# Sums of weight blocks by copies and adding transfers instead of VectorE, in a two-layer decoder trunk

## The chip, the cores and the metric

One core of a Trainium2 chip runs the whole program. The metric is the device time of one execution in microseconds, as the median of several; the kernel before took 2176.65 us (median of 3 runs, 2176.36 to 2177.28). Lower is better. The engines are TensorE (matrix products into PSUM), VectorE and ScalarE (elementwise work), GpSimd, and SyncE, whose queue (SP) issues most transfers. All of a core's transfers run on the same 16 DMA engines.

## The reference, cut to what matters

The program is a trunk of two layers on 1024 tokens of width 1024, in float32. Layer 0 mixes tokens with a gated linear recurrence, layer 1 with stick-breaking attention. Each is followed by a SwiGLU network of inner width 2816, which is the part that this change touches:

```python
def swiglu_ffn(x, w_in, w_out):
    gu = jnp.einsum("bsd,df->bsf", x, w_in)
    h = jax.nn.silu(gu[..., :D_FF]) * gu[..., D_FF:]
    return jnp.einsum("bsf,fd->bsd", h, w_out)
```

Here x is the normalized stream, `w_in` is 1024 x 5632 (gate columns, then up columns) and `w_out` is 2816 x 1024.

## The kernel before

Every float32 operand is split into a high part (a cast to float32r, by ScalarE) and a low part (the rest, by a subtraction on VectorE). A product is three matmuls: high x high, high weight x low input, low weight x high input (`mm3`, lines 141 to 144).

Both products of the network are computed by a Strassen-Winograd scheme (`mix_out_ffn_in`, line 625): inputs and weights are cut into 2 x 2 blocks, and seven products of sums of blocks replace eight. The sums on the input side are formed once per layer in `v_steps` (line 579). The sums on the weight side are formed for each step anew. A step of the first product ("f" step, f = 0 to 21) makes 128 gate columns and the 128 up columns that go with them, for all tokens. Then 13 steps ("v" steps) make the second product.

The class `Weights` (line 668) holds one step's weights. `load_a` and `load_b` bring two raw tiles of 512 KB, ra and rb, from HBM, on SP. Each has two halves: a1 and a2 in ra, b1 and b2 in rb, 128 partitions x 512 columns. The raw tiles come from a pool of three buffers, so the next load waits until an old tile has had its last reader. From the halves come four sums, kept in one buffer each for s1 and s4 and a double-width one for sb, whose halves are called c1 and c2 below:

- `s12` (line 695): s1 = b1 + b2
- `s2` (line 698): c1 = s1 - a1
- `s3` (line 701): c2 = a1 - b1
- `do_s4` (line 704): s4 = c1 - a2

`a_hi`, `b_hi`, `c_hi`, `d_hi` cast the high parts (wah from ra, wbh from sb, wch from s1 and b2, wd from s4) and `a_lo` to `d_lo` subtract for the low parts.

A step runs the seven products in the order 0, 1, 2, 3, 4, 6, 5 (`ORDER`, line 565), four blocks of three matmuls each. Product 0 and 1 use wa, 2 and 4 use wb, 3 and 5 use wc, 6 uses wd. In the f steps from 4 to 19 product 1 is itself done by a smaller scheme of the same kind (`inner_part`), on pairs of steps, whose weight sums `inner_sums` takes from two raw tiles. Each product is evicted from PSUM as it ends (`post`), and the gate (`gate`) and the input sums of the second product (`operands`) follow. The loop of the steps begins at line 1192. In it, w is the step's own weights, nw the next step's, ahead those of the step after. After product k of a step it does, besides evictions:

- before product 0: the low part of w's sb, the high part of s1 and b2
- k = 0: their low parts; k = 2: w's wd, and nw's wah
- k = 3: nw's s1; k = 4: nw's wal, c1, c2; k = 5: nw's wbh and s4
- k = 1 or 3: load of ahead's ra; k = 5: load of ahead's rb

TensorE, ScalarE, VectorE and GpSimd run in the written order in this part of the program. The order on SP is the scheduler's. A queue is served in its order, so an instruction that waits holds those behind it.

Of the kernel before, what the change touches and what calls it, by code (L numbers as in the profile page):

```python
# [12 lines left out]
AF = mybir.ActivationFunctionType  # L13
ALU = mybir.AluOpType
# [15 lines left out]
V_MIX, V_FFN, V_FIN, V_BIN, V_CW, V_CB, V_GB, V_LAM, V_BO = 0, 16, 32, 40, 56, 88, 96, 112, 120  # L30
# [3 lines left out]
def trunk(  # L34
# [21 lines left out]
    nc = tc.nc  # L56
    f32 = lambda t: t.bitcast(F32)
# [38 lines left out]
    vc = cp.tile([P, P], F32, name="vc")  # L96
# [15 lines left out]
    def load_raw(src, shape):  # L112
        raw = rp.tile([P, D], F32, tag="raw", name="raw")
        view = raw if len(shape) == 1 else raw.rearrange("p (a b) -> p a b", a=shape[0])
        nc.sync.dma_start(view, src)
        return raw
# [11 lines left out]
    def cols(w, c0, n=P):  # L128
        return w[:, c0 : c0 + n].rearrange("(k p) c -> p k c", p=P)
# [120 lines left out]
    half = lambda t, n: t[:, n * NB : (n + 1) * NB]  # L250
# [8 lines left out]
    with ExitStack() as st, tc.manual_schedule(engines={E.PE, E.Activation, E.DVE, E.Pool, E.SP}):  # L259
# [49 lines left out]
        ps = pst("vps0")  # L309
# [71 lines left out]
        for r0, r1 in ((0, 32), (32, 64), (64, P)):  # L381
            ps = pst("vps")
            nc.tensor.transpose(ps[:, 0 : r1 - r0], vall[r0:r1, :], ident[r0:r1, r0:r1])
            nc.vector.tensor_copy(vc[:, r0:r1], ps[:, 0 : r1 - r0])
        broadcast_r(sps, "tp", 0)
        row_factors(1)
        wsplit(2)
# [191 lines left out]
    def v_steps(h, v, j, gcol, ta, tb):  # L579
        g1, g2 = (vc[:, gcol + d : gcol + d + 1] for d in (j, j + HK))  # L580
        h11, h12, h21, h22 = h[j][0], h[j][1], h[j + HK][0], h[j + HK][1]
        V = nc.vector
        b12 = rbc[0]

        def direct(i, src, g):
            hi, lo = v[i, j]
            nc.scalar.activation(hi, src, AF.Copy, scale=g)
            V.scalar_tensor_tensor(lo, src, g, f32(hi), op0=ALU.mult, op1=ALU.subtract)

        def summed(i, t):  # L590
            hi, lo = v[i, j]
            nc.scalar.copy(hi, t)
            V.tensor_sub(lo, t, f32(hi))
# [9 lines left out]
        V.scalar_tensor_tensor(tb, h22, g2, ta, op0=ALU.mult, op1=ALU.add)  # L603
        summed(3, ta)
        yield
        summed(2, tb)

        V.scalar_tensor_tensor(ta, h22, g2, b12, op0=ALU.mult, op1=ALU.subtract)
        yield
        summed(4, ta)  # L610
        yield

        V.scalar_tensor_tensor(ta, h21, g2, tb, op0=ALU.mult, op1=ALU.subtract)
        yield
        summed(5, ta)

    def v_last(h, v, j, gcol):
        g2 = vc[:, gcol + j + HK : gcol + j + HK + 1]
# [6 lines left out]
    def mix_out_ffn_in(mix, bias, layer, gnext, outs):  # L625
        w_in = ffn_w_in[layer]
        gcol = V_FFN + layer * ND
        V = nc.vector
        half = lambda t, i: t[:, i * NB : (i + 1) * NB]
# [3 lines left out]
        ta, tb = (sp_.tile([P, NB], F32, name=x) for x in ("ta", "tb"))  # L633
# [34 lines left out]
        class Weights:  # L668
            def __init__(self, load, m=HK, eng=V):
                self.load, self.m, self.eng, self.a = load, m, eng, {}  # L670
                self.ready = False

            def load_a(self):
                self.ra = self.load(0)
# [12 lines left out]
                for i, x in zip(idx, range(2)):  # L687
                    self.a[i] = (half(hi, x), half(lo, x))

            def s12(self):  # L690
# [3 lines left out]
                self.s1, self.s4 = (t[:, 0 : self.m * P] for t in (self.s1, self.s4))  # L694
                self.eng.tensor_add(self.s1, self.part(self.rb, 0), self.part(self.rb, 1))

            def s2(self):
                self.eng.tensor_sub(self.part(self.sb, 0), self.s1, self.part(self.ra, 0))

            def s3(self):  # L700
                self.eng.tensor_sub(self.part(self.sb, 1), self.part(self.ra, 0), self.part(self.rb, 0))  # L701

            def do_s4(self):
                self.eng.tensor_sub(self.s4, self.part(self.sb, 0), self.part(self.ra, 1))

            def a_hi(self):
                self.wa = wtile("wah")
# [45 lines left out]

        def weights_in(f, now=True):
            w = Weights(lambda x: load_raw(cols(w_in, x * DFF + f * P), (ND,)))
            if now:
                w.load_a()
                w.load_b()
            return w
# [11 lines left out]
        with tc.manual_schedule(engines={E.PE, E.Activation, E.DVE, E.Pool}):  # L771
# [11 lines left out]
            w = None  # L783
            for j in range(HK):
                rows = (j, j + HK)
                dn = [(d, n) for d in rows for n in range(NH)] if j else [(d, n) for n in range(NH) for d in rows]
                for k, (d, n) in enumerate(dn):
                    o = HK * j + k
                    if (d, n) in begun:
                        ps = begun[d, n]  # L790
                        hi, lo = mix.w[d]
                        mm3(ps, hi[:, ND - 1], lo[:, ND - 1], xh[ND - 1][n], xl[ND - 1][n], False, True)
                    else:
                        ps = pp.tile([P, NB], F32, tag="p", name="ob_ps")
# [11 lines left out]
                    if o == 10:  # L806
                        w = weights_in(0)
# [40 lines left out]
            def post0(i, ps):  # L848
                g0, g1, u0, u1 = halves(0)
                if i == 0:  # L850
                    nc.scalar.copy(g1, ps)
                elif i == 1:
                    V.tensor_add(g0, ps, g1)
                elif i == 2:
                    V.tensor_add(g1, ps, g1)
                elif i == 4:
                    V.tensor_add(u0, ps, g1)
                elif i == 3:
                    V.tensor_sub(u1, u0, ps)
                    V.tensor_sub(g1, g1, ps)  # L860
                elif i == 5:
                    V.tensor_add(u0, ps, u0)
                else:
                    V.tensor_sub(g1, g1, ps)

            def post(f, i, ps):
                g0, g1, u0, u1 = halves(f)
                if i == 0:  # L870
                    nc.scalar.copy(g0, ps)
                elif i == 1:
                    V.tensor_add(g0, ps, g0)
                elif i == 2:
                    nc.scalar.copy(g1, ps)
                elif i == 3:
                    nc.scalar.copy(u1, ps)
                elif i == 4:
                    nc.scalar.copy(u0, ps)
                    V.tensor_sub(u1, u0, u1)  # L880
                elif i == 6:
                    V.tensor_sub(g1, g1, ps)
                else:
                    nc.scalar.copy(u0, ps)

            def gate(f, k):
                G, U = GT[f % 2], UT[f % 3]
                if k == 0:
                    V.tensor_mul(G, ob, G)
                elif k == 1:  # L890
                    nc.scalar.activation(G, G, AF.Silu)
                elif k == 2:
                    V.tensor_mul(G, ob, G)
                else:
                    V.tensor_mul(U, U, G)
# [111 lines left out]
            ps = half(ob, 0)  # L1007
# [184 lines left out]
            for s_, (kind, x) in enumerate(steps):  # L1192
                w, nw, ahead = nw, nxt, None
# [23 lines left out]
                for k, i in enumerate(ORDER):  # L1217
# [61 lines left out]
                    if k == 0:  # L1279
                        if kind == "v":  # L1280
                            w.c_hi()
                        w.c_lo()
                    elif k == 2:
                        w.d_hi()
                        w.d_lo()
                        if nw:
                            nw.a_hi()
                    elif nw and last_two:
                        if k == 4:
                            nw.a_lo()  # L1290
# [543 lines left out]
```

## Time and profile before

| | before |
|---|---|
| median of 3 runs | 2176.65 us |
| the profiled execution | 2176.2 us |
| its span in the profile | 2174.1 us |
| clock granted to TensorE | 0.999 |
| GpSimd busy | 113.5 us |
| moved by DMA | 294.49 MB, 135 GB/s |

The first products of the network (f = 0 to 21) start on TensorE at 325 us in layer 0 and at 1527 us in layer 1; the v steps start at 726 and 1928 us. The rows that carry the argument are shown with the prediction. In a row of groups stand line, engine, operation, output <- inputs, partitions x elements and type, count, then busy us, mean ns of one, and idle time before it with what ended it. In a row of the timeline stand start and duration in us, engine, line, operation. In a row of transfers the last figure is the median time in us from issue to landing. "SPq" is SP's queue, "PEld" TensorE's weight loads.

### The profile page before, as it was taken

Reading aid. Unit: us, or ns where it says so; the run is one execution under the profiler, and the core shown is the slowest. Engines: PE = TensorE matmul, PEld = TensorE weight load, DVE = VectorE, ACT = ScalarE, POOL = GpSimd, SP = SyncE. Lnnn points to the kernel's source line nnn. Section 1 sums busy time; section 2 is a strip of 40 time slices with the busy share of each in tenths; the row PEclk is TensorE's granted clock in tenths of the full one; section 3 lists DMA queues with packets and bytes.
Section 4 is the critical chain, followed back from the end, with each engine's and each line's share of the span. In section 5 each row is a group of like instructions: output and inputs, shape, how many; then the busy total and the mean of one; then the engine's idle time right before and its main releaser. Section 6 shows DMA issues by size and latency. Waiting matters only on the chain.

```text
span 2174.1 us, 28371 instructions
## 1 busy us (share of the span) xinstructions
PE 2160.4 (99%) x10414; PEld 1810.7 (83%) x10414; DVE 1787.3 (82%) x2604; ACT 1104.9 (51%) x1821; POOL 113.5 (5%) x85
## 2 busy tenths in 40 slices
PE   8999999999999999999999999999999999999998
PEld 7888888888888888888888888888888888888887
DVE  7887778888888887887888888886888888888886
ACT  6667445444444544564555555553544444454556
POOL 1222020000000000000000000001000000000002
PEclk9999999999999999999999999999999999999999
DMA  7111422334345864434333344463133444587442
GB/s 234 49 49 39 160 88 67 113 126 158 132 152 197 271 219 131 146 120 101 101 94 93 99 105 107 139 211 117 59 114 115 154 141 154 172 276 237 136 154 93
DMA packets 305323, 294.49 MB, mean 135 GB/s; under 512 B 16280, under 2 KB 212000, under 8 KB 305184
## 3 DMA queue, kind: packets, MB, share of 16 engines
q1 hardware_dynamic: 305024, 292.42, 42.8%
q8 instruction: 81, 1.33, 0.2%
q14 instruction: 58, 0.48, 0.1%
q10 hardware_dynamic: 160, 0.27, 0.0%
HBM read 184.09 MB, written 83.36 MB: 123 GB/s over the span
## 4 chain that ended last, share of the span: by engine, by line
PE 90%; DVE 5%; ACT 3%; DMA 1%; issue 0%; SPq 0%; DVEq 0%; ACTq 0%
PE p_ps L142 17%; PE p_ps L144 17%; PE p_ps L143 17%; PE qk_ps L142 4%; PE qk_ps L144 4%; PE qk_ps L143 4%; PE wt_ps L1650 3%; PE ob_ps L143 3%; PE ob_ps L142 2%; PE ob_ps L144 2%; PE z_ps L1620 2%; PE z_ps L1621 2%; PE av_ps L1672 2%; PE av_ps L1671 1%; PE i_ps L144 1%; PE i_ps L143 1%
## 5 line engine op out<-in xcount | busy, mean ns | idle before, releaser
L142 PE MATMUL p_ps<-vh,wbh 128*128 128x512 f32 x524 | 204.7, 391 | 0.0
L143 PE MATMUL p_ps<-vl,wbh 128*128 128x512 f32 x524 | 204.5, 390 | 0.0
L142 PE MATMUL p_ps<-vh,wch 128*128 128x512 f32 x524 | 204.2, 390 | 0.0
L144 PE MATMUL p_ps<-vh,wcl 128*128 128x512 f32 x524 | 204.1, 390 | 0.0
L144 PE MATMUL p_ps<-vh,wbl 128*128 128x512 f32 x524 | 204.1, 390 | 0.0
L143 PE MATMUL p_ps<-vl,wch 128*128 128x512 f32 x524 | 203.9, 389 | 0.0
L1659 ACT CAST th<-wt_ps 128x512 fp32r<-128x512 f32 x192 | 92.5, 482 | 209.0 <-PE wt_ps L1650 208.9
L717 ACT CAST wbh<-sb 128x1024 fp32r<-128x1024 f32 (+2 forms) x69 | 69.8, 1012 | 190.4 <-DVE sb L701 190.4
L1660 DVE TENSOR_TENSOR tl<-wt_ps,th 128x512 fp32r<-128x512 f32 x192 | 106.2, 553 | 62.8 <-ACT th L1659 60.9
L144 PE MATMUL p_ps<-vh,wal 128*128 128x512 f32 x396 | 154.3, 390 | 0.1
L143 PE MATMUL p_ps<-vl,wah 128*128 128x512 f32 x396 | 154.1, 389 | 0.0
L142 PE MATMUL p_ps<-vh,wah 128*128 128x512 f32 x396 | 154.1, 389 | 0.0
L142 PE MATMUL qk_ps<-vh,whi 128*128 128x512 f32 x264 | 118.3, 448 | 0.0
L144 PEld LDWEIGHTS p_ps<-vh,wbl 128*128 128x128 f32 x524 | 98.4, 188 | 21.8 <-DVE wbl L721 0.8
L144 PEld LDWEIGHTS p_ps<-vh,wcl 128*128 128x128 f32 x524 | 98.3, 188 | 21.1 <-DVE wcl L731 0.6
L142 PEld LDWEIGHTS p_ps<-vh,wch 128*128 128x128 f32 x524 | 98.4, 188 | 20.6 <-ACT tb L1176 0.2
L143 PEld LDWEIGHTS p_ps<-vl,wch 128*128 128x128 f32 x524 | 98.4, 188 | 20.2
L142 PEld LDWEIGHTS p_ps<-vh,wbh 128*128 128x128 f32 x524 | 98.6, 188 | 19.0
L143 PEld LDWEIGHTS p_ps<-vl,wbh 128*128 128x128 f32 x524 | 98.6, 188 | 18.5
L1636 DVE TENSOR_TENSOR_SCAN w<-w,unit 128x128 f32<-128x128 f32 (+3 forms) x128 | 108.3, 846 | 4.1 <-ACT w L1633 4.1
L144 PE MATMUL qk_ps<-vh,wlo 128*128 128x512 f32 x264 | 104.1, 394 | 0.0
L143 PE MATMUL qk_ps<-vl,whi 128*128 128x512 f32 x264 | 103.5, 392 | 0.0
(390 smaller groups left out, 5929.6 us busy)
## 6 DMA issues: line engine op xcount, KB each, us to landing
raw<-in_ffn_w_in SPq DMA_DIRECT2D x88, 512.0 KB, 3.9
vl<-pd SPq DMA_DIRECT2D x128, 256.0 KB, 3.3
pd<-U SPq DMA_DIRECT2D x90, 256.0 KB, 2.3
kk<-two SPq DMA_DIRECT2D x64, 256.0 KB, 4.2
raw<-in_ffn_w_out SPq DMA_DIRECT2D x56, 256.0 KB, 3.4
raw<-in_attn_w_qkv SPq DMA_DIRECT2D x24, 512.0 KB, 4.1
h<-hd SPq DMA_DIRECT2D x32, 256.0 KB, 5.4
hd<-h SPq DMA_DIRECT2D x32, 256.0 KB, 2.0
```

Of the source, the lines that this page charges most:

```text
L142: nc.tensor.matmul(ps, lhsT=wh, rhs=mh, start=first, stop=False, **kw)
L143: nc.tensor.matmul(ps, lhsT=wh, rhs=ml, start=False, stop=False, **kw)
L144: nc.tensor.matmul(ps, lhsT=wl, rhs=mh, start=False, stop=last, **kw)
L717: nc.scalar.copy(self.full(self.wb), self.full(self.sb))
L1620: nc.tensor.matmul(ps[:, 0 : c1 - c0], lhsT=lhsT, rhs=KK[q][hx][:, 0, c0:c1], start=True, stop=False)
L1621: nc.tensor.matmul(ps[:, 0 : c1 - c0], lhsT=lhsT, rhs=KK[q][hx][:, 1, c0:c1], start=False, stop=True)
L1636: nc.vector.tensor_tensor_scan(rev, rev, unit[:, NB - n :][:, ::-1], 0.0, op0=ALU.mult, op1=ALU.add)
L1650: nc.tensor.transpose(tp[:, c : c + P], W[q, hx, j, kb // 4][:, (kb % 4) * P : (kb % 4 + 1) * P], ident)
L1659: nc.scalar.copy(th[:, q0:], tp[:, q0:])
L1660: nc.vector.tensor_sub(tl[:, q0:], tp[:, q0:], f32(th)[:, q0:])
L1671: nc.tensor.matmul(ps[:, q0:], lhsT=VV[q][:, kb, hx], rhs=th[:, q0:], start=first, stop=False)
L1672: nc.tensor.matmul(ps[:, q0:], lhsT=VV[q][:, kb, hx], rhs=tl[:, q0:], start=False, stop=last)
```

## The change

For the f steps from 2 to 21 the four sums are no longer formed on VectorE. `by_dma` (after product 0 of the step before) has SP copy a1 into both halves of sb, and b1 into s1. Then three transfers issued by GpSimd, which add to their destination, make c2 += b1, s1 += b2 and c1 += s1. `by_dma4` (after product 2) has SP copy a2 into s4, and GpSimd add c1 to it. Since only additions occur, c1, c2 and s4 have other signs than before: c1 = s1 + a1, c2 = a1 + b1, s4 = c1 + a2. Signs elsewhere make up for this: the norm gains of the network are negated once (so the input side and the gate come with the other sign), two of the input sums are stored negated, subtractions after some products become additions, and SiLU is taken with scale -1. The steps f = 0 and f = 1 form their sums on VectorE with the new signs, the v steps as before. In the built program VectorE has 2421 instructions in place of 2581, GpSimd 226 in place of 65, SP 1041 in place of 877, ScalarE 1785 in place of 1784; TensorE's count is the same.

```diff
+        nc.scalar.activation(vc[:, V_FFN:V_FIN], vc[:, V_FFN:V_FIN], AF.Copy, scale=-1.0)
...
-        def summed(i, t):
+        def summed(i, t, minus=False):
             hi, lo = v[i, j]
+            if minus:
+                nc.scalar.activation(hi, t, AF.Copy, scale=-1.0)
+                V.scalar_tensor_tensor(lo, t, -1.0, f32(hi), op0=ALU.mult, op1=ALU.subtract)
+                return
             nc.scalar.copy(hi, t)
             V.tensor_sub(lo, t, f32(hi))
...
-        summed(2, tb)
+        summed(2, tb, True)
...
-        summed(5, ta)
+        summed(5, ta, True)
...
+            def by_dma(self):
+                self.sums()
+                dma = nc.gpsimd.dma_start
+                a1, b1, c1 = (half(t, 0) for t in (self.ra, self.rb, self.sb))
+                b2, c2 = half(self.rb, 1), half(self.sb, 1)
+                nc.sync.dma_start(c1, a1)
+                nc.sync.dma_start(c2, a1)
+                nc.sync.dma_start(self.s1, b1)
+                dma(c2, b1, accum_op=ALU.add)
+                dma(self.s1, b2, accum_op=ALU.add)
+                dma(c1, self.s1, accum_op=ALU.add)
+
+            def by_dma4(self):
+                nc.sync.dma_start(self.s4, half(self.ra, 1))
+                nc.gpsimd.dma_start(self.s4, half(self.sb, 0), accum_op=ALU.add)
...
             def s2(self):
-                self.eng.tensor_sub(self.part(self.sb, 0), self.s1, self.part(self.ra, 0))
+                (self.eng.tensor_add if self.plus else self.eng.tensor_sub)(
+                    self.part(self.sb, 0), self.s1, self.part(self.ra, 0)
+                )
...
-                    V.tensor_sub(u1, u0, u1)
+                    V.tensor_add(u1, u0, u1)
                 elif i == 6:
-                    V.tensor_sub(g1, g1, ps)
+                    V.tensor_add(g1, ps, g1)
...
-                    nc.scalar.activation(G, G, AF.Silu)
+                    nc.scalar.activation(G, G, AF.Silu, scale=-1.0)
...
                         w.c_lo()
+                        if nw and nw.plus:
+                            nw.by_dma()
                     elif k == 2:
                         w.d_hi()
                         w.d_lo()
+                        if nw and nw.plus:
+                            nw.by_dma4()
...
-                        if k == 3:
+                        if k == 3 and not nw.plus:
                             nw.s12()
                         elif k == 4:
                             nw.a_lo()
-                            nw.s2()
-                            nw.s3()
+                            if not nw.plus:
+                                nw.s2()
+                                nw.s3()
                         elif k == 5:
                             nw.b_hi()
-                            nw.do_s4()
+                            if not nw.plus:
+                                nw.do_s4()
```

More of the change, by code (lines that the diff above doesn't have):

```diff
@@ L670, in __init__ @@
                 self.load, self.m, self.eng, self.a = load, m, eng, {}
-                self.ready = False
+                self.ready, self.plus = False, False
             def load_a(self):
@@ L688, in put, with sums @@
                     self.a[i] = (half(hi, x), half(lo, x))
-            def s12(self):
+            def sums(self):
                 self.sb = sp_.tile([P, S], F32, tag="sb", name="sb", bufs=1)
@@ L694, in s12 @@
                 self.s1, self.s4 = (t[:, 0 : self.m * P] for t in (self.s1, self.s4))
+            def by_dma(self):
[12 more added lines that the diff above has]
+                nc.gpsimd.dma_start(self.s4, half(self.sb, 0), accum_op=ALU.add)
+            def s12(self):
+                self.sums()
                 self.eng.tensor_add(self.s1, self.part(self.rb, 0), self.part(self.rb, 1))
             def s2(self):
-                self.eng.tensor_sub(self.part(self.sb, 0), self.s1, self.part(self.ra, 0))
+                (self.eng.tensor_add if self.plus else self.eng.tensor_sub)(
+                    self.part(self.sb, 0), self.s1, self.part(self.ra, 0)
+                )
             def s3(self):
-                self.eng.tensor_sub(self.part(self.sb, 1), self.part(self.ra, 0), self.part(self.rb, 0))
+                (self.eng.tensor_add if self.plus else self.eng.tensor_sub)(
+                    self.part(self.sb, 1), self.part(self.ra, 0), self.part(self.rb, 0)
+                )
             def do_s4(self):
-                self.eng.tensor_sub(self.s4, self.part(self.sb, 0), self.part(self.ra, 1))
+                (self.eng.tensor_add if self.plus else self.eng.tensor_sub)(
+                    self.s4, self.part(self.sb, 0), self.part(self.ra, 1)
+                )
             def a_hi(self):
@@ L755, in weights_in @@
             w = Weights(lambda x: load_raw(cols(w_in, x * DFF + f * P), (ND,)))
+            w.plus = True
             if now:
@@ L858, in post0 @@
                 elif i == 3:
-                    V.tensor_sub(u1, u0, ps)
-                    V.tensor_sub(g1, g1, ps)
+                    V.tensor_add(u1, ps, u0)
+                    V.tensor_add(g1, ps, g1)
                 elif i == 5:
@@ L863, in post0 @@
                 else:
-                    V.tensor_sub(g1, g1, ps)
+                    V.tensor_add(g1, ps, g1)
             def post(f, i, ps):
@@ L879, in post @@
                     nc.scalar.copy(u0, ps)
-                    V.tensor_sub(u1, u0, u1)
+                    V.tensor_add(u1, u0, u1)
                 elif i == 6:
-                    V.tensor_sub(g1, g1, ps)
+                    V.tensor_add(g1, ps, g1)
                 else:
```

## The prediction

> **What bounds the kernel now.** I read the page's busy table first, then the stretches of time in which the w_in steps run, then TensorE's own waits, then one such step instruction by instruction.
>
> ```profile
> span 2174.1 us, 28371 instructions
> PE 2160.4 (99%) x10414; PEld 1810.7 (83%) x10414; DVE 1787.3 (82%) x2604; ACT 1104.9 (51%) x1821; POOL 113.5 (5%) x85
> ```
> ```profile
> 360.00:749.00 389.00, 389.00 (x1881) 328.63 (x1880) 329.26 (x489) 181.38 (x284) 0.00 (x0) 1.00 0.47 155
> 1530.00:1925.00 395.00, 394.93 (x1915) 333.67 (x1914) 332.39 (x496) 181.37 (x280) 0.00 (x0) 1.00 0.42 139
> ```
>
> The second fence gives, per stretch, the busy time of TensorE, its weight loads, VectorE, ScalarE and GpSimd, then the granted clock, the DMA share and GB/s. The two stretches are the w_in steps of the two layers. TensorE has no gap, VectorE is busy 85%, GpSimd does nothing.
>
> ```profile
> 1664.16 0.39 PE L142 MATMUL p_ps<-vh,wah 128*128 128x512 f32 x1
> 1664.39 0.39 PE L143 MATMUL p_ps<-vl,wah 128*128 128x512 f32 x1
> 1666.88 0.28 PE L142 MATMUL i_ps<-ith,ish 128*128 128x256 f32 x1
> 1682.66 0.39 PE L142 MATMUL p_ps<-vh,wah 128*128 128x512 f32 x1
> 1686.82 0.40 PE L142 MATMUL p_ps<-vh,wbh 128*128 128x512 f32 x1
> ```
> ```profile
> PEld p_ps L144 <- DVE wal L712: 1.0, 2, 0.5
> PEld p_ps L144 <- DVE wbl L721: 0.8, 2, 0.4
> PEld p_ps L144 <- DVE wcl L731: 0.6, 2, 0.4
> ```
>
> These are starts in TensorE's timeline. The first product of a step is 12 matmuls in 1666.88 - 1664.16 = 2.72 us, 0.227 us each; one step starts at 1664.16, the next at 1682.66. "Busy" could hide gaps, since ends are modelled, but an even pitch of starts can't. In all the span weight loads waited 2.4 us for VectorE's low parts, in six places. So there is next to nothing to win here: VectorE isn't the bound, and the question is whether the new path is quick enough to stay hidden.
>
> **What is removed.** Twenty w_in steps per layer (f 2 to 21; f 0 and 1 keep VectorE) lose four operations each, 160 in all.
>
> ```profile
> L695 DVE TENSOR_TENSOR s<-raw 128x512 f32<-128x512 f32 x58 | 40.5, 698 | 0.0
> L704 DVE TENSOR_TENSOR s<-sb,raw 128x512 f32<-128x512 f32 x58 | 39.9, 687 | 0.0
> L698 DVE TENSOR_TENSOR sb<-s,raw 128x512 f32<-128x512 f32 x58 | 39.8, 686 | 0.1
> L701 DVE TENSOR_TENSOR sb<-raw 128x512 f32<-128x512 f32 x58 | 39.8, 685 | 0.0
> ```
>
> 40 x (0.698 + 0.687 + 0.686 + 0.685) = 110 us less on VectorE. On the path that sets the end it is worth 0, by TensorE's even pitch; at most the 2.4 us above.
>
> **The signs.** They change operations, not counts or shapes: subtractions into additions, a copy into a scaled copy. Sixteen low parts (L593, 0.69 us) become scalar_tensor_tensor (0.75 us by L603), 16 x 0.06 = 1 us of VectorE, hidden by TensorE; without that cover it is 1 us. The negated gains cost one small ScalarE operation near the start (0.3 us by the 128x4 activation). Both at 0.
>
> ```profile
> L603 DVE SCALAR_TENSOR_TENSOR tb<-h,vc,ta 128x512 f32<-128x512 f32 x8 | 6.0, 746 | 0.1
> L593 DVE TENSOR_TENSOR vl<-tb,vh 128x512 fp32r<-128x512 f32 x8 | 5.5, 693 | 0.7
> L180 ACT ACTIVATE rs_s<-ssum,eps 128x4 f32<-128x4 f32 x2 | 0.6, 299 | 0.0
> ```
>
> **What is added: a chain of transfers.** Per step SP issues copies c1, c2, s1 after product 0 and s4 after product 2; GpSimd issues c2 += b1, s1 += b2, c1 += s1, s4 += c1. All are 256 KB. What is summed in step f is used in step f + 1. s1 copy, s1 += b2, c1 += s1 follow each other, and only then is sb whole; s4 += c1 is a fourth link. The next step's c1 overwrites sb, which s4 += c1 reads, so SP waits for it: four links make a loop that must fit into one step. No accumulating transfer stands in the trace, so I price it from the nearest rows.
>
> ```profile
> kk<-two SPq DMA_DIRECT2D x64, 256.0 KB, 4.2
> vl<-pd SPq DMA_DIRECT2D x128, 256.0 KB, 3.3
> hd<-h SPq DMA_DIRECT2D x32, 256.0 KB, 2.0
> raw<-in_ffn_w_in SPq DMA_DIRECT2D x88, 512.0 KB, 3.9
> g<-hd SPq DMA_DIRECT2D x32, 256.0 KB, 5.6
> q1 hardware_dynamic: 305024, 292.42, 42.8%
> ```
> ```profile
> L379 POOL COPY vall<-vraw 128x128 f32<-128x128 f32 x1 | 0.3, 291 | 7.4 <-DMA vraw<-in_lru_b_out 7.4
> 1664.44 0.38 SPq L115 DMA_DIRECT2D raw<-in_ffn_w_in  x1
> 1660.15 1.22 DVE L712 TENSOR_TENSOR wal<-raw,wah 128x1024 fp32r<-128x1024 f32 x1
> 1697.89 1.22 DVE L712 TENSOR_TENSOR wal<-raw,wah 128x1024 fp32r<-128x1024 f32 x1
> 1681.11 1.06 ACT L717 CAST wbh<-sb 128x1024 fp32r<-128x1024 f32 x1 [3.10 <-DVE sb L701]
> 1685.06 1.22 DVE L721 TENSOR_TENSOR wbl<-sb,wbh 128x1024 fp32r<-128x1024 f32 x1
> ```
>
> Step length: the two L712 rows lie two steps apart, (1697.89 - 1660.15)/2 = 18.87 us. One accumulate: 4.2 us (kk<-two, the only SBUF to SBUF transfer of this size), plus a second read, since the destination is an operand too: 42.8% of 2174.1 us for 292.42 MB is 0.83 us per 256 KB; plus 0.3 us of GpSimd to start it (L379). Sum 5.3 us. Bounds: 2.0 (hd<-h, a lone transfer) and 8.4 (kk<-two twice). I take 5.3, as kk<-two is the nearest in kind. From c1's issue to s1 landed: two more issues of 0.4 and 3.3 (vl<-pd, issued in series) = 4.1; bounds 2.8 and 5.0 with 2.0 and 4.2 for the landing.
>
> Loop: 4.1 + 3 x 5.3 = 20.0 us against 18.87: 1.13 us too long per step. By the low bounds it is 2.8 + 6.0 = 8.8 us and costs nothing, by the high ones 5.0 + 25.2 = 30.2 and every step would be 11 us longer. Slack before TensorE notices: rb lands at 1664.44 + 3.9 = 1668.34, s1 at 1671.64, sb at 1682.24. wbh is wanted at 1686.82 and wbl two matmuls later, 1687.28; less 1.06 (L717) and 1.22 (L721), sb may come at 1685.0. Slack 2.8 us per layer. Loss: 2 x (20 x 1.13 - 2.8) = 39.6 us.
>
> Queued behind the new waits. On SP, behind c1: the next load of raw weights (wanted by the inner sums at product 3), s4, the stores of U and its sums, the load of rb for the step after; they are all late only if the loop is. On GpSimd: nothing (0.00 busy above). On ScalarE, behind wbh: the eviction of product 6 and wch, then on VectorE wcl, which frees s1. Moved earlier: the load of rb no longer waits for the L704 subtraction, only for L712; worth 1 us at most of the slack.
>
> VectorE's entries in the steps between 1660 and 1700 us are TENSOR_TENSOR throughout, like the L712 and L721 rows. The Trainium skill, "SBUF — State Buffer", section "Who interferes with whom", warns that a DMA of GpSimd's queue starves while VectorE runs in a 2-port mode, but names copies, casts and tensor_scalar for it. By that rule these steps pay nothing for it; if it held for TENSOR_TENSOR it would be the third rival below.
>
> **Sum.** 2176.2 us was the profiled run (span 2174.1 plus 2.1 around it), 0.45 below the median 2176.65. 2176.65 + 39.6 = 2216 us.
>
> **Rivals.**
> 1. The chain fits: not slower. The point is an accumulate of (18.87 - 4.1)/3 = 4.92 us, only 0.4 below my value; hd<-h at 2.0 speaks for it, kk<-two at 4.2 with a second read against. Then TensorE keeps its pitch: 2176.5 us. The Trainium skill, "DMA: Bandwidth & Descriptors", section "Anatomy of one DMA — SWDGE (gpsimd) path", fits 2.0 us + bytes/436e3 for this queue; with both operands read that is an estimate of 3.2 us, and the loop 13.7 us. No run here shows that queue.
> 2. The 16 DMA engines become the bound. Share 0.47 x 18.87 = 8.9 us a step, plus four copies of 0.83, plus four accumulates of three passes, 10.0: 22.2 us, 3.3 too long: 40 x 3.3 - 5.6 = 126 us, 2303 us. With two passes it is 18.9, just even. Against it: 0.83 is a mean with many small packets.
> 3. Each accumulate's start waits for a VectorE instruction, up to 1.22 us (L712): accumulate 6.5, loop 23.6, 4.7 too long: 182 us, 2359 us.
> 4. Only the layer's last steps lose, where 16 reloads of h (g<-hd, 32 in two layers, 5.6 us to landing where 3.3 is usual) pass the same engines: three of 0.83 before each of two accumulates is 5.0 us against 2.8 of slack: 2 x 2.2, 2181 us.
> 5. Faster: all 2.4 us of the weight loads' waits vanish and something like it elsewhere: 2174 us. VectorE's relief speaks for it, the even pitch against.
>
> **How the numbers follow.** The chain is too long: 0.50, of which 0.08 lies above 2400 (an accumulate over 6.8 us; at 8.4 the loop is 29.3 and the time 2588). Rival 1: 0.29. Rival 2: 0.08. Rival 3: 0.06. Rival 4: 0.04. Rival 5: 0.03. Prediction 2216 us. The forecast's own range is 2181 to 2400; with rival 1 it becomes 2174 to 2400. 0.2% is 4.4 us, about what a measurement of this kernel can tell from no change. Slower: 0.50 + 0.08 + 0.06 + 0.04 = 0.68; same 0.29; faster 0.03.
>
> **What would show it.** Right: gaps in TensorE ahead of wbh in most w_in steps, wbh (ScalarE) waiting for a DMA into sb, SP waiting for s4 += c1, a step near 20 us. Rival 1: an even 0.227 us pitch and accumulates landing under 4.9 us. Rival 2: a DMA share near 1. Rival 3: accumulates starting as VectorE's instructions end. VectorE must lose 160 instructions and some 110 us in any case. I am wrong if TensorE keeps its pitch, or if the gaps lie elsewhere than ahead of wbh and the products after it.

## The result, and the profile after

The changed kernel takes 2269.09 us (median of 4 runs, 2262.33 to 2272.12) against 2176.51 us (median of 4, 2176.04 to 2177.28) for the kernel before: ratio 1.0421, 95% interval 1.0396 to 1.0445, slower by some 93 us. The profiled execution took 2262.33 us, 86.1 more than the one of before. One figure above is wrong: the v steps of the kernel before start on TensorE at 745 and 1947 us; 726 and 1928 us are the starts of f = 21.

From the page of the kernel after, the span, the busy table and GpSimd's DMA queue (packets, MB, share of the 16 engines' span); then its stretches (busy time of TensorE, weight loads, VectorE, ScalarE, GpSimd, granted clock, DMA share, GB/s) for the step f = 2, the steps 3 to 18 and the step 20 of layer 0; then its waits (engine, line waited for: us in total, times, longest).

```profile
span 2260.6 us, 29098 instructions
PE 2187.9 (97%) x10414; PEld 1823.0 (81%) x10414; DVE 1695.0 (75%) x2444; ACT 1096.1 (48%) x1822; POOL 252.4 (11%) x245
q0 software_dynamic: 23040, 41.95, 11.1%
```
```profile
365.10:391.60 26.50, 22.08 (x86) 17.25 (x85) 16.61 (x21) 12.42 (x18) 4.38 (x5) 0.87 0.61 165
391.60:718.90 327.30, 309.17 (x1484) 259.65 (x1483) 220.37 (x325) 131.34 (x207) 54.13 (x62) 0.99 0.84 227
740.80:768.10 27.30, 21.16 (x85) 16.99 (x85) 12.73 (x16) 7.75 (x12) 4.35 (x5) 0.87 0.94 297
```
```profile
PE p_ps L142 <- ACT G L902: 52.4, 29, 6.1
ACT wbh L747 <- DMA sb<-s: 268.8, 40, 13.3
SPq L706 <- DMA s<-sb: 188.1, 36, 8.6
POOL sb L711 <- DMA s<-raw: 215.5, 40, 9.2
```

TensorE, without a gap before, now stands still in the w_in steps. Of the 86 us, some 59 are idle time (span minus busy: 72.7 us against 13.7) and 27.5 are a longer busy time, most of it matmuls that last longer at a lower granted clock (0.87 in the first and the last of these rows). The waits name the links. wbh waits in all 40 steps for the adding transfer that ends c1 (sb<-s), c1's own transfer waits in all 40 for s1, and SP's copy for the next step waits in 36 for s4 += c1 (s<-sb). That last line is the loop. VectorE lost its 160 instructions, but 92 us of busy time rather than 110.

TensorE's own wait carries the name of an eviction (ScalarE, line 902). One turn of the kernel after in its timeline shows why. (Lines after: 706 c1 copy, 710 s1 += b2, 711 c1 += s1, 715 s4 += c1, 747 wbh, 756 and 757 wch, 902 the eviction of product 0.)

```profile
522.90 0.47 SPq L706 DMA_DIRECT2D sb<-raw  x1
...
528.01 0.89 POOL L710 DMA_DIRECT2D s<-raw  x1
534.78 0.87 POOL L711 DMA_DIRECT2D sb<-s  x1 [5.88 <-DMA s<-raw]
538.71 1.05 ACT L747 CAST wbh<-sb 128x1024 fp32r<-128x1024 f32 x1 [8.02 <-DMA sb<-s]
539.26 0.86 POOL L715 DMA_DIRECT2D s<-sb  x1 [3.61 <-DVE G L920]
...
540.14 0.62 ACT L756 CAST wch<-s 128x512 fp32r<-128x512 f32 x1
540.66 0.62 ACT L757 CAST wch<-raw 128x512 fp32r<-128x512 f32 x1
541.18 0.59 ACT L902 COPY G<-p_ps 128x512 f32<-128x512 f32 x1
541.82 0.50 PE L142 MATMUL p_ps<-vh,wbh 128*128 128x512 f32 x1 [2.14 <-ACT G L902]
543.66 0.47 SPq L706 DMA_DIRECT2D sb<-raw  x1
```

The turn from one c1 copy to the next takes 543.66 - 522.90 = 20.76 us: 5.11 us to s1 += b2, 6.77 for that link, 4.48 for c1 += s1 up to the start of s4 += c1, 4.40 for s4 += c1. When sb is whole at last, ScalarE works off its queue in order (wbh, an eviction, wch twice), and only then product 0's eviction, which frees the PSUM bank that product 2 uses again: 541.82 - 538.71 = 3.1 us after sb. The line that a wait names is the last in a row of things, not the first.

The same copies at the start and the end of seventeen turns of each layer, from the timeline of the kernel after:

```profile
376.03 0.47 SPq L706 DMA_DIRECT2D sb<-raw  x1
...
728.27 0.47 SPq L706 DMA_DIRECT2D sb<-raw  x1
...
1624.14 0.47 SPq L706 DMA_DIRECT2D sb<-raw  x1
...
1969.43 0.47 SPq L706 DMA_DIRECT2D sb<-raw  x1
```

(728.27 - 376.03)/17 = 20.72 us in layer 0 and (1969.43 - 1624.14)/17 = 20.31 us in layer 1, 20.52 in the mean, against a step of 18.87 us before.

### The profile page after: what moved, and what is told of

It is laid out like the page before. It is cut to its first block, busy times and chain, and to the rows that moved or that the text cites. A ratio compares the mean times of both kernels' runs of the same rounds, so it can differ in the third digit from the quotient of the medians.

```text
span 2260.6 us, 29098 instructions
## 1 busy us (share of the span) xinstructions
PE 2187.9 (97%) x10414; PEld 1823.0 (81%) x10414; DVE 1695.0 (75%) x2444; ACT 1096.1 (48%) x1822; POOL 252.4 (11%) x245
## 3 DMA queue, kind: packets, MB, share of 16 engines
q0 software_dynamic: 23040, 41.95, 11.1%
## 5 line engine op out<-in xcount | busy, mean ns | idle before, releaser
L142 PE MATMUL p_ps<-vh,wbh 128*128 128x512 f32 x524 | 215.0, 410 | 52.4 <-ACT G L902 52.4
L144 PE MATMUL p_ps<-vh,wbl 128*128 128x512 f32 x524 | 211.5, 404 | 4.7 <-DVE wbl L751 4.7
L143 PE MATMUL p_ps<-vl,wbh 128*128 128x512 f32 x524 | 211.2, 403 | 0.0
L751 DVE TENSOR_TENSOR wbl<-sb,wbh 128x1024 fp32r<-128x1024 f32 (+2 forms) x69 | 83.1, 1205 | 108.9 <-ACT wbh L747 107.6
L143 PEld LDWEIGHTS p_ps<-vl,wbh 128*128 128x128 f32 x524 | 102.4, 195 | 19.7
```

Source lines behind the costliest of these rows:

```text
L142: nc.tensor.matmul(ps, lhsT=wh, rhs=mh, start=first, stop=False, **kw)
L143: nc.tensor.matmul(ps, lhsT=wh, rhs=ml, start=False, stop=False, **kw)
L144: nc.tensor.matmul(ps, lhsT=wl, rhs=mh, start=False, stop=last, **kw)
L751: V.tensor_sub(self.full(lo), self.full(self.sb), self.full(f32(self.wb)))
```

## The experiments

The table compares each kernel's steps with those of the kernel before, from its profiled execution: the length of a step is the time between the first matmuls of product 0 in it and in the next, and the figures are the sums of what is over, both layers together. The first columns are medians and ratios to the kernel before, with 95% intervals.

| kernel | us | ratio (95%) | f = 2 | f = 3 to 19 | f = 20 | f = 21, v |
|---|---|---|---|---|---|---|
| after | 2269.09 | 1.0421 (1.0396 to 1.0445) | 14.3 | 50.6 | 15.0 | 6.8 |
| e1_signs_only | 2176.43 | 0.9999 (0.9990 to 1.0009) | 0 | 0 | 0 | 0 |
| e2_mid_only | 2240.39 | 1.0297 (1.0280 to 1.0314) | 0 | 57.4 | 0 | 0 |
| e3_unlinked | 2208.55 | 1.0145 (1.0130 to 1.0160) | 13.9 | 8.5 | 6.1 | 0 |
| e4_s1_first | 2237.64 | 1.0273 (1.0251 to 1.0296) | 14.1 | 34.6 | 14.1 | 0.2 |
| e5_wch_later | 2270.76 | 1.0439 (1.0424 to 1.0455) | 13.6 | 54.8 | 16.7 | 9.7 |
| e6_no_adding | 2179.75 | 1.0021 (1.0012 to 1.0031) | 1.7 | 0 | 0 | 1.8 |
| e7_c2_vector | 2205.25 | 1.0139 (1.0124 to 1.0154) | 11.1 | 5.6 | 6.2 | 3.8 |
| e8_combined | 2185.69 | 1.0050 (1.0035 to 1.0065) | 0 | 9.4 | 0 | 0 |
| e9_s4_only | 2190.87 | 1.0068 (1.0053 to 1.0083) | 0 | 15.5 | 0 | 0 |
| e10_s4_vector | 2195.53 | 1.0087 (1.0071 to 1.0102) | 8.3 | 0 | 7.0 | 4.4 |
| e11_two_links | 2176.93 | 1.0006 (0.9996 to 1.0015) | 0 | 0 | 0 | 0 |
| e12_s4_plain | 2178.42 | 1.0009 (0.9999 to 1.0019) | 0 | 1.6 | 0 | 0 |

**The signs alone.** All sums go back to VectorE, the new signs stay: a flag of its own, in all five conditions of the loop, decides on the transfers.

```diff
+            w.dma = False
...
-                        if nw and nw.plus:
+                        if nw and nw.dma:
                             nw.by_dma()
...
-                            if not nw.plus:
+                            if not nw.dma:
                                 nw.s2()
                                 nw.s3()
```

> The four sums back on VectorE, with the new signs; no copies or adding transfers. Theory (the whole loss is the chain of transfers): the time of before, 2176.5 us within 1, no wait of TensorE in the w_in steps. Rival (the sign edits or the negated gains cost part of the 92 us): clearly above 2180 us.

It measured as the kernel before. The signs cost nothing that shows, and the whole loss belongs to the transfers.

**The middle steps alone.** The same flag with `w.dma = 3 <= f <= 19`: the first and the last steps keep VectorE.

> Transfers for the weights of f = 3 to 19 only; f = 2, 20 and 21 form their sums on VectorE. In the changed kernel's trace the steps f = 2 are 7 us longer than before in each layer, f = 20 and 21 and the first v step together some 11 us. Theory (these ends are lost on top of the loop): about 36 us less than the changed kernel, near 2233 us, with the steps in between as long as they were. Rival (the ends only collect a delay that the loop in between has built up): the loss stays above 80 us, near 2260 us.

The losses of f = 2, 20 and 21 vanish, those of the middle stay (57.4 against 50.6). The time is 7 us above the theory's 2233 and 20 below the rival's 2260. The kernel after is 29 us slower than this one, so the ends are worth some 29 us of the 93. The last steps are no alternative to the slow loop, as the prediction's fourth rival had it; they come on top.

**One link cut.** s4's adding transfer takes b1, not c1, so that it need not wait for c1 and the next c1 copy need not wait for it; every byte still moves.

```diff
-                nc.gpsimd.dma_start(self.s4, half(self.sb, 0), accum_op=ALU.add)
+                nc.gpsimd.dma_start(self.s4, half(self.rb, 0), accum_op=ALU.add)
```

> The last adding transfer adds b1 to s4 in place of c1, so the output is another, but every transfer keeps its size and place. The next copy into sb no longer waits for it. Theory (a loop of four links, 20.4 us, against a step of 18.87): SP's wait ahead of the copies into sb vanishes, sb comes about 15.5 us after the step's start and the steps f = 3 to 19 lose nothing; only the ends stay, 2210 to 2225 us. Rival (the 16 DMA engines, at a share of 0.80 to 0.96, are the bound): the bytes are the same, so the time stays at 2260 to 2270 us.

The wait of this kernel that answers to the first of the kernel after:

```profile
PE p_ps L142 <- ACT G L902: 15.1, 12, 3.0
```

The middle loses 8.5 us in place of 50.6 with the same transfers on the same engines; the theory had nothing for it, and its 2210 us are missed by 1.5. So the middle is for the most part the loop's, not the DMA engines': from 391 to 719 us they are busier here (share 0.90) than in the kernel after (0.84 in the row above). In five of the eight waits that are left in the middle (f = 9, 11, 13 and 17), the eviction of product 0 had itself waited for a store of G; the run with only s4 by transfers, below, comes back to it.

**The links in another order.** s1 is copied first, and s1 += b2 goes ahead of c2 += b1.

```diff
+                nc.sync.dma_start(self.s1, b1)
                 nc.sync.dma_start(c1, a1)
                 nc.sync.dma_start(c2, a1)
-                nc.sync.dma_start(self.s1, b1)
-                dma(c2, b1, accum_op=ALU.add)
                 dma(self.s1, b2, accum_op=ALU.add)
+                dma(c2, b1, accum_op=ALU.add)
                 dma(c1, self.s1, accum_op=ALU.add)
```

> The same transfers in another order: s1 is copied first, s1 += b2 is issued ahead of c2 += b1. In the changed kernel s1 += b2 starts 4.5 us after the first copy's issue and takes a median of 6.1 us beside its sibling, where 3.3 is the least. Theory (the loop): the chain is 2 to 3 us shorter, a loop of about 18 us, so the steps in between lose next to nothing: 2215 to 2230 us. Rival (the DMA engines' share): unchanged, 2260 to 2270 us.

This won less than was expected, and 2237.64 us lies between the theory and the rival. s1 += b2 became shorter (a median of 3.8 us to landing in the middle turns, 5.9 in the kernel after), but s4 += c1 became longer (5.5 in place of 4.3), and the turn shrank only from 20.5 to 20.1 us. Time that is won in one link was here partly paid in the next. What made s4 += c1 longer is not shown. The loss now falls mostly in odd steps: in 12 of the middle's 14 waits of TensorE the eviction of product 0 had waited for the store of G (7 of 23 in the kernel after, most of them for about 0.5 us).

**What stands between wbh and the eviction.** wch is cast after the eviction of product 0.

```diff
-                    if kind == "f":
-                        w.c_hi()
...
-                        if kind == "v":
+                        if kind == "v" or s_:
                             w.c_hi()
```

> The changed kernel, but ScalarE's cast wch is done after the eviction of product 0 instead of before it (steps after the first). Theory, the loop of four links sets the pace: TensorE's wait for that eviction ends about 1.0 us earlier once per layer, and every later step still waits for the chain; 2260 to 2268 us, the middle steps (f = 3 to 19) still 45 to 52 us over before. Rival, every wait is made dear by what stands between wbh and that eviction: 1.0 us less in each of some 34 stalled steps, and fewer halved clocks; 2225 to 2235 us.

Nothing was won; the time is a little above the theory's bounds and its interval overlaps that of the kernel after, and the rival is out. That fits a loop that sets the pace: a shorter way from the loop to TensorE would then be worth its length once per layer, not once per step, and the 2 us of two layers are lost in the spread.

**The adding taken out.** The four transfers on GpSimd's queue become plain copies.

```diff
-                dma(c2, b1, accum_op=ALU.add)
-                dma(self.s1, b2, accum_op=ALU.add)
-                dma(c1, self.s1, accum_op=ALU.add)
+                dma(c2, b1)
+                dma(self.s1, b2)
+                dma(c1, self.s1)
...
-                nc.gpsimd.dma_start(self.s4, half(self.sb, 0), accum_op=ALU.add)
+                nc.gpsimd.dma_start(self.s4, half(self.sb, 0))
```

> The changed kernel with GpSimd's four transfers per step as plain copies on the same queue, to the same places, with the same bytes; nothing is added, so the sums of the steps f = 2 to 21 are not formed. If the adding costs a second read, as the prediction sized it (0.83 us each), three links become 2.5 us shorter, the loop 18 us, and only the layers' first and last steps lose: 2205 to 2225 us. If the price is that of GpSimd's queue and of sharing the engines, the links stay as they are: 2255 to 2275 us, with landings of c1 += s1 still 4 to 4.5 us in the median.

Both expectations missed: 2179.75 us is below either. For the kernel after, the transfers of GpSimd's queue that lie in the loop (count, KB each, median us from issue to landing) and what GpSimd spent on issuing one kind of them:

```profile
s<-raw POOLq DMA_DIRECT2D x40, 256.0 KB, 6.1
sb<-s POOLq DMA_DIRECT2D x40, 256.0 KB, 4.3
s<-sb POOLq DMA_DIRECT2D x40, 256.0 KB, 4.4
```
```profile
L711 POOL DMA_DIRECT2D sb<-s x40 | 34.7, 868 | 215.5 <-DMA s<-raw 215.5
```

The same views of the kernel without adding, and its row of GpSimd's queue:

```profile
s<-raw POOLq DMA_DIRECT2D x40, 256.0 KB, 2.8
sb<-s POOLq DMA_DIRECT2D x40, 256.0 KB, 2.9
s<-sb POOLq DMA_DIRECT2D x40, 256.0 KB, 2.8
```
```profile
L711 POOL DMA_DIRECT2D sb<-s x40 | 21.6, 539 | 127.9 <-DMA s<-raw 127.9
q0 software_dynamic: 12800, 41.95, 5.1%
```

Same queue, same bytes, same links, and hardly a loss (3.9 us): it is the adding that is dear. It takes 1.4 (4.3 against 2.9) to 3.3 us (6.1 against 2.8) of a link that lies in the loop, and 0.33 us more of GpSimd for each issue. Of the time of all 16 engines an adding transfer occupies 11.1% of 2260.6 us / 160 = 1.57 us, a plain one 5.1% of 2175.8 us / 160 = 0.69 us, in 144 packets against 80. The second read that the prediction put at 0.83 us is there as engine time (1.57 - 0.69 = 0.88), but the time to landing grows by more than that.

The Trainium skill, "Collectives: The Full Stack", section "The bandwidth ceiling: the fold count and why AG ≠ RS ≠ AR", says of the adding step of a collective that it costs not by its addition but by its two source reads, twice the read traffic per byte. The engine time here, 2.3 times that of a copy, agrees, and somewhat more.

**Fewer transfers, the same links.** c2 goes back to VectorE, 80 transfers fall away.

```diff
-                nc.sync.dma_start(c2, a1)
...
-                dma(c2, b1, accum_op=ALU.add)
...
                             if not nw.plus:
                                 nw.s2()
-                                nw.s3()
+                            nw.s3()
```

> The changed kernel with c2 = a1 + b1 back on VectorE (40 operations of 0.69 us), so 80 transfers fewer; the four links stay. Theory, links are long where they share the engines with a sibling: s1 += b2 starts about 1.5 us earlier and alone (3.5 to 4.5 us instead of 6), the loop is about 17 us, the middle steps lose under 10 us, the first and last steps of a layer still lose some 20 to 30: 2200 to 2215 us. Rival, the links do not depend on the sibling: the loop is 18.5 to 20 us, 2225 to 2250 us.

As the theory said. The transfers of GpSimd's queue in this kernel:

```profile
s<-raw POOLq DMA_DIRECT2D x40, 256.0 KB, 3.4
sb<-s POOLq DMA_DIRECT2D x40, 256.0 KB, 3.9
s<-sb POOLq DMA_DIRECT2D x40, 256.0 KB, 4.9
```

s1 += b2, alone on the engines, lands after 3.4 us in place of 6.1, and the middle loses 5.6 us in place of 50.6. So up to 2.7 us of that link's time came with its sibling c2 += b1, issued just before it, on which nothing in the loop depends. It isn't the sibling alone: in the next kernel, which keeps the sibling and has no transfers for s4, the same link lands after 4.3 us.

**The fourth link undone.** s4 = c1 + a2 goes back to VectorE; c1, c2 and s1 stay with the transfers.

```diff
-                        if nw and nw.plus:
-                            nw.by_dma4()
...
-                            if not nw.plus:
-                                nw.do_s4()
+                            nw.do_s4()
```

> The changed kernel with s4 = c1 + a2 back on VectorE after wbh (40 operations of 0.69 us), so without the fourth link; c1, c2 and s1 still come from transfers. Theory, the four links in a loop set the pace of the middle steps: with three links the next c1 copy waits only for VectorE, the chain of some 16 us fits into a step, the middle steps (f = 3 to 19) lose under 10 us in all, the first and last steps of a layer still lose 15 to 30: 2190 to 2212 us. Rival, s1 += b2 and c1 += s1 alone are late in every step, because they start only after product 0: the middle steps still lose 20 us or more, over 2220 us.

The middle loses nothing at all, with c2 += b1 still beside s1 += b2. So a chain of three links fits, the loop of four doesn't; removing one link is enough for the middle, and removing one sibling nearly so. With s4's transfers more than a link is gone, though: the store of G lands after 2.2 us here and after 4.7 in the kernel after. What is left (19.7 us) is all at the ends.

**Putting the cures together.** First f = 3 to 19 only, c2 on VectorE and wch later (e8); then f = 3 to 19 only, c2 and s4 on VectorE, so that s1 and c1 alone come from transfers (e11).

> The path by transfers only for f = 3 to 19, c2 on VectorE, wch cast after the eviction of product 0. Theory, nothing is left that is late: 2177 to 2187 us, under 10 us over before, no halved clock. If the transfers cost by their mere share of the 16 engines, over 2195 us.

> Transfers only for f = 3 to 19, and only for s1 and c1 (copies, s1 += b2, c1 += s1); c2 and s4 on VectorE. Theory, nothing is late and no loop is left: 2175 to 2179 us, no step over before by more than 0.5 us, though 68 of VectorE's 160 operations are still gone. If adding transfers cost TensorE something even when they are in time, over 2182 us.

e8 keeps its four links and still loses 9.4 us, within the time expected, but something is late, and after one wait the clock is lower (0.79 from 1748 to 1756 us). Its turns, 16.4 to 21.8 us in layer 1, show a loop near the edge. The waits that reach TensorE tell another story; product 0's eviction is line 901 here:

```profile
PE p_ps L142 <- ACT G L901: 6.2, 6, 2.3
ACT G L901 <- DMA pd<-G: 36.0, 14, 5.8
```

Each of the six stands behind an eviction that had waited for the store of G. How the 9.4 us divide between the loop and that store no run separates. e11 has no loop and is equal to the kernel before, with 68 of VectorE's operations gone. That is the best that was found, and it wins nothing, for VectorE wasn't the bound.

**One link off the loop.** Only s4 by transfers, for all steps, the rest on VectorE.

```diff
-                        if nw and nw.plus:
-                            nw.by_dma()
...
                             nw.a_lo()
-                            if not nw.plus:
-                                nw.s2()
-                                nw.s3()
+                            nw.s2()
+                            nw.s3()
+                            if nw.dma:
+                                nw.by_dma4()
```

> Only s4 comes from transfers (a copy by SP and one adding transfer, both issued after VectorE's c1 and c2 in product 4), for all steps f = 2 to 21; 40 operations fewer on VectorE. s4 is wanted only in product 6 of the next step, after products 0 to 4. Theory, one link that is off the loop costs nothing, and VectorE's relief wins nothing: 2175 to 2179 us. Rival, the copy waits for the previous step's wd and holds SP's loads behind it: over 2185 us.

A miss: some 15 us over, in odd steps of the middle only. The time is the rival's, the cause isn't, as will be seen. The wait that is new in this kernel, the wait of TensorE that goes with it, and its store of G:

```profile
ACT G L903 <- DMA pd<-G: 49.1, 17, 4.3
PE p_ps L142 <- ACT G L903: 10.7, 17, 1.8
```
```profile
pd<-G SPq DMA_DIRECT2D x22, 256.0 KB, 5.8
```

The store of G and the same row of the kernel before:

```profile
pd<-G SPq DMA_DIRECT2D x22, 256.0 KB, 2.0
```

Product 0's eviction writes G, which a store still reads, and the store lands after 5.8 us in place of 2.0. It is issued when it was, mostly 0.96 us before its step begins, so SP isn't held up. But two transfers now start 0.6 us ahead of it. One is the adding transfer, as soon as c1 and c2 stand. The other is the load of 512 KB of raw weights. In the kernel before, the last reader of the raw tile was VectorE's s4 (line 704, for which 41 of these loads waited), and the load came behind the store; without that reader it goes ahead. SP at the step f = 7 of layer 1, in the kernel before and in this one:

```profile
1663.20 0.32 SPq L903 DMA_DIRECT2D pd<-G  x1
1664.44 0.38 SPq L115 DMA_DIRECT2D raw<-in_ffn_w_in  x1
```
```profile
1671.68 0.38 SPq L115 DMA_DIRECT2D raw<-in_ffn_w_in  x1
1672.24 0.45 SPq L935 DMA_DIRECT2D pd<-G  x1
```

So even a transfer that nobody waits for can be paid by one that somebody waits for. The last run makes the adding transfer a plain copy (`accum_op` left out) and leaves the load where it is.

> The kernel with only s4 by transfers, with GpSimd's transfer as a plain copy of c1 (a2 is not added, so s4 is not the reference's sum). With the adding transfer the odd steps lost 0.5 to 2 us each, where the store of G landed after 5.8 us instead of 2.0 and the eviction of product 0 waited for it. Theory, the adding transfer's second read on the shared engines makes that store late: with a plain copy the store of G lands in under 4.5 us, no step is over before by more than 0.3 us, 2175 to 2179 us. Rival, any transfer of 256 KB at that moment does it: the store still takes over 5 us and the kernel 2185 us or more.

Its store of G and its wait for it:

```profile
pd<-G SPq DMA_DIRECT2D x22, 256.0 KB, 4.9
```
```profile
ACT G L903 <- DMA pd<-G: 31.0, 14, 2.7
```

The time is as the theory had it; the store isn't (4.9, not under 4.5), and one step is 0.5 us over. Some 3 of the 4 us that the store is late are there without the adding, and ScalarE waits for it too (31.0 us in place of 49.1), but of TensorE's waits behind that eviction one of 0.2 us is left. The 0.9 us that the adding puts on top is what reached it. Of the 3 us, 2.4 need no transfer of GpSimd's at all. In the kernel without adding (e6) one of these is issued at 456.35 us and lands after 2.3 us, and the next is issued at 466.18 us. The store of G between them, behind the load, lands after 4.4 us:

```profile
458.46 0.38 SPq L115 DMA_DIRECT2D raw<-in_ffn_w_in  x1
459.01 0.45 SPq L934 DMA_DIRECT2D pd<-G  x1
```
```profile
pd<-G SPq DMA_DIRECT2D x1, 256.0 KB, 4.4
```

No run put the load back behind the store and left s4 to the transfers.

## Why the prediction was right in direction and wrong in size

**The bound and the place.** Right. TensorE was the bound and VectorE's relief is worth nothing: e11 gives 68 operations away and gains 0. The loop of four links, wbh waiting for sb, SP waiting for s4 += c1 and a step near 20 us are all in the trace. VectorE's 110 us were counted from durations, which overlap with the next instruction's; two operations of the kernel before, back to back:

```profile
553.32 0.69 DVE L698 TENSOR_TENSOR sb<-s,raw 128x512 f32<-128x512 f32 x1
553.92 0.69 DVE L701 TENSOR_TENSOR sb<-raw 128x512 f32<-128x512 f32 x1
```

They start 0.60 us apart, and 160 x 0.60 = 96 us is near the 92 measured.

**The signs, GpSimd, and what is queued behind.** The signs are right at 0 (e1). The place where TensorE waits was another one: not wbh itself but product 0's eviction behind wbh and wch on ScalarE, 3.1 us after sb, not the 1.8 (1686.82 - 1685.0) of the prediction. That took 1.3 us from the slack of a layer; by e5 such a piece is lost in the spread. On SP the prediction saw that the load of rb moves earlier and called it a gain of 1 us at most. It didn't see that the load thereby overtakes the store of G, for which product 0's eviction waits. In the kernel after this is small (ScalarE waits 7.4 us for it, 9 times), but it is the last wait in most of what e7, e8 and e9 lose in the middle.

**The failed step is the last line of the sum: "Loss: 2 x (20 x 1.13 - 2.8) = 39.6 us."** It takes all twenty steps of a layer for turns of one and the same loop. The profiled execution lost 86.7 us in these steps, in two parts.

- The seventeen middle steps: forecast 2 x (17 x 1.13 - 2.8) = 32.8 us, measured 50.6, of which 42 go with the fourth link (e3). The turn was well sized, 20.52 us against 20.0, but the loss is the small difference between turn and step: 0.5 us more is 1.65 in place of 1.13 per step, 34 x 0.52 = 18 us in all.
- The steps f = 2, 20, 21 and v: forecast 6 x 1.13 = 6.8 us, measured 36.1. Here the chain isn't in its steady turn. At f = 20 and 21 it shares the engines with the 16 reloads of h (the share is 0.94 in the stretch of f = 20 shown above): that is the prediction's fourth rival, which it put beside the loop as another way to go, at 4.4 us for both layers; e2 shows that the loss there comes on top, with 21.8 us. That the reloads are its cause is argued: no run moved them. In the step f = 2 the first chain starts late and lands late; the prediction gave it only its turn's 2 x 1.13 us, and it lost 14.3. Without adding (e6) both ends are nearly gone (3.5 us left), so both are for the most part the price of adding transfers on shared engines; for f = 2 no run separates the late start from the long links.

**The price of one adding transfer, 5.3 us.** Right in the mean (6.77, 4.48 and 4.40 us in the turn shown, 5.2), by two errors that cancel, so by luck. Its base, kk<-two at 4.2 us, is too dear: a plain copy on this queue lands after 2.8 to 3.0 us here. Its second read, 0.83 us, is too cheap: the adding puts 1.1 us on the shortest landing (3.3 against 2.2 in the two kernels below) and 1.4 to 3.3 on the medians. The lines are the shortest, median and longest time to landing of c1 += s1, first in the kernel after, then in the one without adding.

```profile
DMA to landing us min/median/max: 3.3/4.3/6.9
```
```profile
DMA to landing us min/median/max: 2.2/2.9/6.6
```

The Trainium skill, "DMA: Bandwidth & Descriptors", section "Anatomy of one DMA — SWDGE (gpsimd) path", gave the prediction an estimate of 3.2 us with both operands read. The trace agrees for the shortest landing (3.3 us), and not for the median (4.3).

**The head, 4.1 us.** Near: 4.5 us in the median of the middle turns from the c1 copy to s1 += b2, since c2 += b1 is issued by GpSimd first.

**The rivals.** The first, that the chain fits, is out by the middle's 50.6 us; e10 shows how near it was: with one link less it holds. The second, DMA engines as the bound, is out by e3 and e10. The third, starts that wait for VectorE, is out by the issue times: 0.868 us in the mean for c1 += s1, with 0.859 the shortest and 0.885 the longest, beside a VectorE that is busy 67% (220.37 of 327.30 us). The fifth is out.

**The clock.** Not in the sum at all. After some of the gaps the granted clock falls to half. Two stretches of the kernel after, the first 1.4 us behind such a gap, the second right after it:

```profile
480.00:483.40 3.40, 3.40 (x10) 2.66 (x9) 1.89 (x4) 0.32 (x1) 0.00 (x0) 0.51 0.65 239
484.00:494.00 10.00, 10.00 (x46) 8.29 (x45) 7.84 (x12) 3.69 (x6) 2.62 (x3) 1.00 0.80 187
```

Counted by their starts, the slow matmuls of the middle steps last 11.6 us longer than at the usual 0.227 us. There it probably adds little to the time, since the loop's turn goes on while TensorE is slow and the next wait can be shorter by as much; this is argued, not shown. In the steps f = 2 and f = 20, where matmuls start more than 0.3 us apart with no wait between them, what they are over 0.227 us comes to 2.5 + 3.0 + 1.9 + 2.9 = 10.3 us, a part of the 29.3 us lost there. No run took the clock's part out by itself.

## What to carry to other kernels

A chain of transfers that must turn once per step is to be costed as a loop, and its loss is the difference of two large numbers: forecast it with its spread, and cost the first turn and the last ones separately, where loads or reloads share the engines. Count the engine time of an adding transfer as that of two to three copies of the same bytes, expect it to land later when it runs beside others, and put it neither in a loop nor next to a store that an eviction waits for. When an instruction is taken away, ask which transfer had waited for it, and what that transfer will now overtake. Before any of this, ask whether the engine that is relieved was the bound; if it wasn't, the best that can come out is no change.

## What the runs showed of the hardware that was not expected

An adding transfer of 256 KB between SBUF tiles takes 144 packets and 1.57 us of engine time against 80 packets and 0.69 us for a copy, and GpSimd spends 0.87 us in place of 0.54 on its issue. Two that run beside each other land later than one alone: s1 += b2 takes 6.1 us in the kernel after and 4.3 in e10, both with its sibling, against 3.4 without it (e7).

A store of 256 KB behind a load of 512 KB that was issued 0.55 us ahead of it landed after 4.4 us in place of 2.0, in a step of e6 with no transfer of GpSimd's on the way.

TensorE's clock fell after short gaps. In the kernel after, one of 1.87 us was enough, as the timeline shows, and matmuls of 0.39 us took 0.63:

```profile
1864.78 0.50 PE L142 MATMUL p_ps<-vh,wbh 128*128 128x512 f32 x1 [1.87 <-ACT G L902]
...
1865.88 0.63 PE L143 MATMUL p_ps<-vl,wbh 128*128 128x512 f32 x1
```

The Trainium skill, "TensorE: Matmul & The Clock Gate", section "Why this matters for your kernels", warns of idle gaps over some 3 us. Here 1.87 us did it, in a stream that is dense otherwise, though not each gap of that length did: after the one of 2.14 us at 541.82 us the matmuls kept their pitch.
